# Sixty matrix products on constant tiles, appended at the end of a two-layer hybrid trunk

## The chip, the core and the metric

The kernel runs on one core of a Trainium2 chip. The metric is the device time of one execution in microseconds, as the median over executions of the program. A separate, profiled execution gives the trace; its span runs from the first to the last instruction, and its device time is somewhat longer than its span.

A core has a matrix engine (TensorE, PE in the profile; its weight loads stand in a row of their own, PEld), a vector engine (VectorE, DVE), an activation engine (ScalarE, ACT), a general engine (GpSimd, POOL) and one that issues transfers (SyncE, SP). ACT, POOL and SP issue DMA transfers here. A product reads a stationary operand (the weights that are loaded into the array, one column for each row of the output) and a moving operand that streams through, both from the on-chip memory SBUF, and writes or adds into a bank of the accumulator memory PSUM (512 fp32 values in each of 128 partitions).

## The reference

Two layers over 256 tokens of 2048 channels in fp32. Each has a convolution branch and an attention branch, both read from one input projection, merged by sigmoid gates and put through an output projection.

```python
def hybrid_layer(x, cos, sin, norm_g, w_in, ...):
    h = rmsnorm(x, norm_g)
    proj = h @ w_in
    (c_a, c_glu, c_gate, q_down, kv_down, k_pe, m_gate,
     g_conv, g_mla) = jnp.split(proj, idx, axis=-1)
    y_conv = conv_branch(c_a, c_glu, c_gate, ...) @ w_proj_conv
    y_mla = mla_branch(q_down, kv_down, k_pe, m_gate, cos, sin, ...) @ w_proj_mla
    y = jax.nn.sigmoid(g_conv) * y_conv + jax.nn.sigmoid(g_mla) * y_mla
    return x + y @ w_out
```

The appended products compute nothing of this: they read tiles of ones, and what they write into PSUM is read by nobody.

## The kernel before

Every large product splits each fp32 number into a high and a low part of type fp32r (`F32R` in the code) and adds three partial products: high by high, low by high, high by low. Weights come in pieces of 128 x 2 x 512 values (`raw`), ACT rounds them to `hi`, VectorE subtracts to get `lo`, and TensorE runs twelve products for a piece: two halves of the tokens, two blocks of 128 channels, three parts. The stationary operand is a 128 x 128 block of the activations (`h_hi`, `h_lo`, later `oT`, `ycT`, `yT`), the moving operand a 128 x 512 block of the weights. An instruction `matmul` on fp32r brings its own weight load, so each product is one MATMUL and one LDWEIGHTS in the profile.

The function `trunk` issues all of it. The wrapper `InOrder` around each engine (`pe`, `vec`, `act`, `gps`, `sp`) ties every instruction to the one issued before it on the same engine, so each engine runs its instructions in the order of the code. As all of them go through the wrapper's inner function `issue`, nearly all lines of the profile say L135. A step that belongs beside the products is put at a slot (`at_slot`, `late`, `fill`) and issued when `product` has issued the piece of that slot. The last kind of block is `wout`: four blocks of 512 output channels, 48 products of 128 x 512 for each half of the tokens. `wout_evac` of the last layer adds PSUM to the residual in `xres` on VectorE, 256 columns at a time; for the last block SP and ACT issue the output transfers. After `trunk` the program closes (L1407): SP waits for the last events of all engines and transfers, and then the engines meet.

Tiles come from pools that rotate over a fixed number of buffers for each tag: `uv` has nine buffers of 128 x 572 values, `big` six of 128 x 4096, and `s0` and `s1` one PSUM bank each, used by the attention scores. A new tile of a tag takes the oldest buffer of it and waits for its last readers.

Three things in the kernel are related to the appended work. At the very start, nineteen products `warm` of 256 columns run on a constant zero (both operands read one constant element, broadcast), and their result is never read. The score products `s` of the attention read both operands from one tile, `qk_t`. And the first block of the first layer takes its first two pieces in single blocks, so TensorE waits there between products.

Of the kernel before, what the change touches and what calls it, by code (L numbers as in the profile page):

```python
# [11 lines left out]
F32 = mybir.dt.float32  # L12
F32R = mybir.dt.float32r
# [6 lines left out]
P = 128  # L20
T = 2
SEQ = 256
# [4 lines left out]
PAD = CONV_W - 1  # L27
# [96 lines left out]
def trunk(ctx: ExitStack, tc: tile.TileContext, xT, x, g_in, pos, win, wuq, wukv, wpc, wpm, wo, cst, rows, invf, out):  # L124
# [411 lines left out]
    for l in range(DEPTH):  # L536
# [763 lines left out]
        if not last_layer:  # L1300
            h_hi, h_lo = keep["h"]

def _blocked(w, widths):
# [105 lines left out]
```

## Time and profile before

| | |
|---|---|
| median of 2 runs | 1876.24 us (1876.01 to 1876.46) |
| profiled execution | 1876.45 us |
| its span | 1874.7 us |
| granted TensorE clock, mean | 1.000 |
| matrix products, weight loads | 8571, 8571 |
| PE busy, of the span | 1869.2 us |
| VectorE busy, of the span | 1577.5 us |

Times are in microseconds unless marked ns. Lines of a group give the line of code, the engine, the operation, the tile written and the tiles read, the shapes, a count, and then the busy time, the mean duration of one in ns, and the idle time of the engine just before them with what ended it. The duration of a product is longer than the distance to the next one, because products are pipelined: the rate is read from the starts. In the chain of waits a line gives its start, its length and what it was; the timeline gives the same for each engine, with runs of like instructions merged and their count behind an x. In a table of windows each engine's busy time stands with its number of instructions, then the granted clock (1.00 is full speed), the share of the DMA engines and GB/s.

### The profile page before, as it was taken

How to read it: one execution, taken by the hardware profiler on the slowest of the kernel's cores; microseconds unless marked ns; L12 is line 12 of the kernel's file. 1: busy time of each engine (PE TensorE's matmuls, PEld its weight loads, DVE VectorE, ACT ScalarE, POOL GpSimd, SP SyncE). 2: the span in 40 equal slices, each digit the busy share in tenths (PEclk: the TensorE clock that was granted, in tenths of full speed). 3: DMA queues.
4: the chain of work that ended last, by engine and by line, in shares of the span. 5: the costliest groups of instructions: out<-in, count | busy, mean ns of one | idle time of the engine just before them, and what ended most of it. 6: DMA issues, size and time to landing. Idle time of an engine off the chain costs nothing.

```text
span 1874.7 us, 27153 instructions
## 1 busy us (share of the span) xinstructions
PE 1869.2 (100%) x8571; PEld 1570.0 (84%) x8571; DVE 1577.5 (84%) x2452; ACT 1358.2 (72%) x2510; POOL 493.7 (26%) x942
## 2 busy tenths in 40 slices
PE   9999999999999999999999999999999999999999
PEld 8988888888888888888899888888888888888887
DVE  6899998898999988766679899889899999885664
ACT  7678888888888876644557688788889888574442
POOL 1055555542200000122221455555322000001210
PEclk9999999999999999999999999999999999999999
DMA  9677777787755566678876777777777556566775
GB/s 327 218 261 257 263 255 256 259 275 232 235 203 193 198 205 218 207 240 277 291 233 218 257 268 254 261 255 269 256 237 242 192 192 204 208 205 223 237 251 164
DMA packets 138961, 445.05 MB, mean 237 GB/s; under 512 B 23681, under 2 KB 29313, under 8 KB 138817
## 3 DMA queue, kind: packets, MB, share of 16 engines
q1 hardware_dynamic: 105120, 359.89, 57.0%
q0 software_dynamic: 32832, 82.62, 13.8%
q8 instruction: 67, 1.10, 0.2%
q10 hardware_dynamic: 864, 0.80, 0.2%
q14 instruction: 78, 0.63, 0.1%
HBM read 399.18 MB, written 44.04 MB: 236 GB/s over the span
## 4 chain that ended last, share of the span: by engine, by line
PE 99%; DMA 1%; ACT 0%; DVE 0%; DVEq 0%; SPq 0%; issue 0%
PE acc L135 97%; PE s L135 2%; PE o_ps L135 1%; DMA raw<-in_win 0%; DMA gx<-in_g 0%; ACT hi L135 0%; PE var L135 0%; PE mu L135 0%; DVE xres L135 0%; DVEq L1407 0%; SPq L135 0%
## 5 line engine op out<-in xcount | busy, mean ns | idle before, releaser
L135 ACT CAST hi<-raw 128x1024 fp32r<-128x1024 f32 (+3 forms) x682 | 699.3, 1032 | 407.4 <-PE acc L135 350.3
L135 DVE TENSOR_TENSOR lo<-raw,hi 128x1024 fp32r<-128x1024 f32 (+3 forms) x682 | 814.1, 1195 | 192.7 <-PE acc L135 146.6
L135 PE MATMUL acc<-hi,hT 128*128 128x512 f32 (+2 forms) x1728 | 419.6, 382 | 0.0
L135 PEld LDWEIGHTS acc<-hi,hT 128*128 128x128 f32 x1728 | 319.6, 188 | 59.1
L135 PE MATMUL acc<-hi,h_hi 128*128 128x512 f32 (+2 forms) x864 | 260.5, 383 | 0.9 <-ACT hi L135 0.9
L135 PE MATMUL acc<-hi,h_lo 128*128 128x512 f32 (+2 forms) x864 | 260.1, 382 | 0.0
L135 ACT ACTIVATE tap<-u_t,cst 128x256 f32<-128x256 f32 x542 | 235.2, 499 | 2.8 <-DVE v_t L135 2.8
L135 PE MATMUL acc<-lo,h_hi 128*128 128x512 f32 (+2 forms) x864 | 229.7, 382 | 0.0
L135 PE MATMUL acc<-lo,hT 128*128 128x512 f32 (+2 forms) x864 | 229.3, 382 | 0.0
L135 DVE TENSOR_TENSOR v_t<-v_t,tap 128x512 f32<-128x512 f32 x271 | 186.3, 688 | 9.7 <-DVE v_t L135 0.9
L135 POOL DMA_DIRECT2D turned<-turn_d x88 | 49.2, 560 | 530.6 <-DVE v_t L135 311.8
L135 PEld LDWEIGHTS acc<-hi,h_lo 128*128 128x128 f32 x864 | 161.0, 188 | 30.2
L135 PEld LDWEIGHTS acc<-lo,h_hi 128*128 128x128 f32 x864 | 160.5, 188 | 30.2 <-DVE lo L135 0.3
L135 PEld LDWEIGHTS acc<-lo,hT 128*128 128x128 f32 x864 | 160.6, 188 | 30.0
L135 PEld LDWEIGHTS acc<-hi,h_hi 128*128 128x128 f32 x864 | 159.9, 188 | 30.6 <-ACT hi L135 1.9
L135 DVE SCALAR_TENSOR_TENSOR v_t<-u_t,cst,v_t 128x256 f32<-128x256 f32 x418 | 178.3, 479 | 2.0
L135 POOL DMA_DIRECT2D turn_d<-gate x184 | 100.2, 552 | 292.9 <-DVE gate L135 176.6
L135 PE MATMUL acc<-hi,oT 128*128 128x512 f32 x512 | 127.8, 389 | 0.0
L135 PE MATMUL acc<-hi,ycT 128*128 128x512 f32 x512 | 127.7, 389 | 0.0
L135 PE MATMUL acc<-hi,yT 128*128 128x512 f32 x512 | 127.7, 389 | 0.0
L135 PE MATMUL acc<-hi,qkc 128*128 128x512 f32 x448 | 115.4, 389 | 0.0
L135 PEld LDWEIGHTS acc<-hi,ycT 128*128 128x128 f32 x512 | 96.1, 188 | 20.0
(171 smaller groups left out, 2221.6 us busy)
## 6 DMA issues: line engine op xcount, KB each, us to landing
raw<-in_win SPq DMA_DIRECT2D x382, 512.0 KB, 4.1
raw<-in_wpm SPq DMA_DIRECT2D x64, 512.0 KB, 3.3
raw<-in_wpc SPq DMA_DIRECT2D x64, 512.0 KB, 4.2
raw<-in_wo SPq DMA_DIRECT2D x64, 512.0 KB, 4.8
raw<-in_wukv SPq DMA_DIRECT2D x32, 512.0 KB, 4.3
turned<-turn_d POOLq DMA_DIRECT2D x56, 256.0 KB, 4.7
raw<-in_win SPq DMA_DIRECT2D x32, 384.0 KB, 4.3
raw<-in_wuq SPq DMA_DIRECT2D x24, 512.0 KB, 4.4
```

The costliest lines, as they stand in the source:

```text
L135: ins = getattr(self.engine, name)(*a, **k)
```

## The change

Behind the last layer, still inside `trunk`, two tiles are taken and filled with ones by VectorE: `near`, a `uv` tile, and `far`, a `big` tile, of which the first 1024 and the last 1024 columns are written. Two PSUM banks are taken under the tags `s0` and `s1`. Then ten groups of six products follow, each with 512 moving columns:

1. weights `near`, 128 columns, banks in turn
2. the same, all six adding into one bank
3. weights of 64 columns, at a named place in the array, output in 64 partitions
4. the same with 32 columns and 32 partitions
5. weights one column of `near`, broadcast to 128
6. moving operand one column of `far`, broadcast to 512
7. both broadcast
8. weights in `far`, 3072 columns from the moving operand
9. weights in `far`, the first 128 of the moving columns themselves
10. weights in `far`, right behind the moving columns

Nothing else differs.

```diff
         if not last_layer:
             h_hi, h_lo = keep["h"]
 
+    near = uv_p.tile([P, 2, PAD + SEQ], F32R, tag="uv", name="near").rearrange("p j n -> p (j n)")
+    far = big.tile([P, 4096], F32R, tag="big", name="far")
+    vec.memset(near.bitcast(F32), 1.0)
+    vec.memset(far[:, :1024].bitcast(F32), 1.0)
+    vec.memset(far[:, 3072:].bitcast(F32), 1.0)
+    banks = [s_p.tile([P, 512], F32, tag=f"s{i}", name=f"bank{i}") for i in range(2)]
+    one, row = near[:, :1].broadcast_to([P, P]), far[:, :1].broadcast_to([P, 512])
+    there = far[:, 3072 : 3072 + P]
+
+    def six(stationary, moving, rows=P, chained=False):
+        kw = {} if rows == P else {"tile_position": (0, 0)}
+        for n in range(6):
+            pe.matmul(banks[0 if chained else n % 2][:rows], stationary, moving,
+                      start=n == 0 or not chained, stop=n == 5 or not chained, **kw)
+
+    six(near[:, :P], far[:, :512])
+    six(near[:, :P], far[:, :512], chained=True)
+    six(near[:, :64], far[:, :512], rows=64)
+    six(near[:, :32], far[:, :512], rows=32)
+    six(one, far[:, :512])
+    six(near[:, :P], row)
+    six(one, row)
+    six(there, far[:, :512])
+    six(far[:, :P], far[:, :512])
+    six(far[:, 512 : 512 + P], far[:, :512])
```

## The prediction

> **What bounds the kernel now.** I read the totals of the page first, then the chain of waits, then the last microseconds of the timeline.
>
> ```profile
> span 1874.7 us, 27153 instructions
> PE 1869.2 (100%) x8571; PEld 1570.0 (84%) x8571; DVE 1577.5 (84%) x2452; ACT 1358.2 (72%) x2510; POOL 493.7 (26%) x942
> PE 99%; DMA 1%; ACT 0%; DVE 0%; DVEq 0%; SPq 0%; issue 0%
> ...
> 10.56 1.05 ACT hi L135
> 11.66 164.66 PE acc L135 x804
> ...
> 257.84 24.50 PE acc L135 x108
> ...
> 1639.66 231.22 PE acc L135 x1020
> 1870.91 0.42 DVE xres L135
> 1871.34 0.33 DVEq L1407
> ```
>
> TensorE is the chain: 99% of it, from 11.66 us to the last output product. There is no gap on it into which sixty more products could be put, and they are issued behind the last one anyway. So the question is only what the end of the kernel looks like, because everything before it stays as it is.
>
> ```profile
> start us, us, engine line op out<-in xcount [idle before <-releaser]
> 1870.26 0.61 PE L135 MATMUL acc<-lo,yT 128*128 128x512 f32 x2
> 1870.46 1.24 SPq L135 DMA_DIRECT2D out<-xres  x2
> 1870.79 1.26 ACTq L135 DMA_DIRECT2D out<-xres  x2
> 1870.91 0.76 DVE L135 TENSOR_TENSOR xres<-acc,xres 128x256 f32<-128x256 f32 x2 [0.15 <-PE acc L135]
> ...
> L135 ACTq DMA_DIRECT2D out<-xres x2: 350/350/351, 1870.8 to 1871.7; - x2
> DMA to landing us min/median/max: 1.9/2.0/2.1
> ...
> L1407 SPq EVENT_SEMAPHORE  x12: 17/28/28, 1871.7 to 1874.6; - x12
> L1407 POOLq EVENT_SEMAPHORE  x4: 17/17/17, 1873.9 to 1874.5; - x4
> ```
>
> The first five lines are the timeline of the last microseconds; then come the page of the tile `xres` and the page of line 1407, which closes the program. TensorE is done at 1870.26 + 0.61 = 1870.87. VectorE adds the last block by 1870.91 + 0.76 = 1871.67. The last output transfer is issued at 1871.7 and lands 2.0 later, at 1873.7. Line 1407 waits for everything, then the engines meet: 1874.7 − 1873.7 = **1.0 us of closing** after the last event that it waits for. TensorE has nothing to do from 1870.87 on, and that tail is what the added work grows out of.
>
> **The change, part by part.** No DMA is added, so no queue of SP, ACT or POOL has anything behind it; the two output issues of SP and ACT stand ahead of all of this and only need the adds. Nothing is removed, and the new tiles have the sizes of the tiles whose buffers they take.
>
> *Three memsets on VectorE*, 572, 1024 and 1024 elements a partition. They are issued after the last add, so they begin at 1871.67. The first products read `near` and the first half of `far`, so TensorE waits for two of the three. No memset this wide is in the trace; these rows bound it:
>
> ```profile
> L135 DVE MEMSET ones<- 128x128 f32 x1 | 0.2, 165 | 0.8 <-PEq L1400 0.8
> L135 DVE MEMSET ss_base<- 128x4 f32 x2 | 0.1, 62 | 0.0
> L135 DVE COPY s1c<-v_t 128x512 f32<-128x512 f32 x2 | 0.9, 428 | 0.1
> L135 DVE CAST parts<-s1c 128x256 fp32r<-128x256 f32 x2 | 0.6, 294 | 0.1
> L135 DVE TENSOR_TENSOR lo<-raw,hi 128x1024 fp32r<-128x1024 f32 x630 | 767.8, 1220 | 172.6 <-PE acc L135 129.3 <-issue 20.3 <-ACT hi L135 9.9
> L135 DVE TENSOR_TENSOR lo<-raw,hi 128x512 fp32r<-128x512 f32 x4 | 2.8, 690 | 0.0
> ```
>
> The two memsets give (165 − 62) / 124 = 0.83 ns an element over a base of 62 ns: 62 + 568 × 0.83 = 533 ns for `near` and 62 + 1020 × 0.83 = 909 ns for half of `far`, 1.44 us together. The copies are faster an element, (428 − 294) / 256 = 0.52 ns, which makes 0.36 + 0.59 = 0.95 us; the subtractions slower, (1220 − 690) / 512 = 1.04 ns, which makes 0.65 + 1.12 = 1.77 us. I take 1.44, since it is the operation itself, and keep both ends. The third memset, 0.9 us, lies beside the first 42 products (over 9 us of TensorE work); only the eighth group reads it, so it costs nothing, and 0.9 us if that cover were gone.
>
> TensorE then starts 0.05 us after the second memset, as it did at 11.66 after ACT's 10.56 + 1.05 = 11.61: 1871.67 + 1.44 + 0.05 = 1873.16.
>
> *The sixty products.* All are 512 columns wide except that the output of twelve has fewer rows. The 108 products from 257.84 us took 24.50 us, 226.9 ns each, with a weight load for every one of them. What can differ is the operands:
>
> ```profile
> L135 PE MATMUL acc<-hi,yT 128*128 128x512 f32 x512 | 127.7, 389 | 0.0
> L135 PEld LDWEIGHTS acc<-hi,yT 128*128 128x128 f32 x512 | 96.1, 188 | 19.9
> 4.21 0.50 PE L135 MATMUL warm<-const-float32-0.0 128*128 128x256 f32 x3
> L135 PE MATMUL warm<-const-float32-0.0 x3: 273/274/274, 4.2 to 4.4; 128*128 128x256 f32 x3
> 283.35 0.88 PE L135 MATMUL s<-qk_t 128*128 128x256 f32 x6
> L135 PE MATMUL s<-qk_t x8: 278/283/288, 283.1 to 283.9; 128*128 128x256 f32 x8
> 11.66 0.73 PE L135 MATMUL acc<-hi,h_hi 128*128 128x512 f32 x2 [0.38 <-ACT hi L135]
> 12.23 0.40 PE L135 MATMUL acc<-hi,h_lo 128*128 128x512 f32 x1
> ```
>
> A load takes 188 ns and lies wholly beside the product before it, so 64 or 32 columns in place of 128 shorten something that is hidden. The score products `s` have both operands in one tile, `qk_t`: (0.88 − 0.283) / 5 = 119 ns for 256 columns. The `warm` products have one constant as both operands, a broadcast that overlaps itself: (0.50 − 0.274) / 2 = 113 ns, 6 ns less. From 256 to 512 columns an interval grows from 119 to 227, 108 ns, so 512 columns are 215 ns of streaming and some 12 ns of something else, which is all that a narrow load or a broadcast could save. Five of the ten groups have one: 30 × 12 ns = 0.36 us at the most. I take 0 and keep 0.36 for the low end. Groups eight to ten (weights in the tile of the moving operand: far away, overlapping, next to it) I cost as the plain ones by the `s` and `warm` rows; if such reads did collide so far that the load was exposed, 188 ns × 18 = 3.4 us would come on top.
>
> The narrow groups are the one thing without a row: the outputs of 64 and 32 rows name a place in the array, so there are three changes of shape (128 to 64, to 32, back). A change costs nothing if the array doesn't care; if it empties first, a product outlasts the next one's start by 389 − 227 = 162 ns, and with the next load exposed as well 162 + 188 = 350 ns. That makes 0, 0.49 or 1.05 us for three. I take 0.25, the middle of the first two, as the loads of every row here overlap. The Trainium skill (TensorEngine Tiling, Key Properties) has a rule against it: changing the tiling mode drains the engine. By that rule alone the sum would be 0.24 us higher, and no trace here shows such a change.
>
> Sum: 59 intervals × 0.2269 = 13.39 us; the first product after a wait has a slower start, 0.73 us for the first pair at 11.66 against 0.61 for the pair at 1870.26, so 0.12; the last one runs its 0.389 to the end; 0.25 for the changes. 14.15 us from 1873.16 gives 1887.31. The closing then takes its 1.0 us: **1888.3, that is 13.6 us more span.** The output transfers have landed by 1873.7, far inside.
>
> The profiled execution took 1876.45 us with this span, so the changed one takes 1890.05. Its 1876.45 is 0.21 above the median of the runs, 1876.24; I forecast **1890.0 us**.
>
> **The rivals.** *The clock drops in the gap.* TensorE stands still from 1870.87 to 1873.16, 2.3 us, the longest gap in the program.
>
> ```profile
> core 0: us, PE busy (x) PEld busy (x) DVE busy (x) ACT busy (x) POOL busy (x), PEclk, DMA share, GB/s
> 1870.90:1874.50 3.60, 0.00 (x0) 0.00 (x0) 0.76 (x2) 0.00 (x0) 0.00 (x0) 1.00 0.44 146
> 1874.60:1874.70 0.10, 0.00 (x0) 0.00 (x0) 0.00 (x0) 0.00 (x0) 0.00 (x0) 0.50 0.00 0
> ...
> 0.75:4.00 3.25, 3.22 (x15) 3.25 (x16) 1.00 0.57 131
> ```
>
> At the end of the old kernel the granted clock was still 1.00 at 1874.50 and 0.50 at 1874.60, some 3.7 us after the last product. With 2.3 us the gap stays short of that, unless the drop comes at fixed times and counts a partly idle stretch. The first `warm` products show the price of a slow array: 3.22 us for 15 of 256 columns is 215 ns each, twice the 113. So one stretch of 3.3 us at that rate would hold 7 to 8 of the new products and cost 0.2 us each: +1.6 us, two stretches +3.1 us, giving 1891.6 to 1893.1. The Trainium skill (TensorE: Matmul & The Clock Gate, Why this matters for your kernels) asks for no idle gap above about 3 us, which agrees with the 3.7 us here and also clears this gap.
>
> *The narrow outputs lose the single pass.* If an output that doesn't fill the array made TensorE run a product in four passes, twelve products would gain three streams of 215 ns: 12 × 0.645 = +7.7 us, 1897.7. For it: no narrow product is in the trace. Against it: nothing else about type or width changes.
>
> *All sixty run in four passes* and the kernel ends slower by over 2%: 60 × 0.645 = +38.7, 1928.7. It decides from the point where 2% (37.5 us, about what a measurement of this kernel can tell from no change) is passed: 1890.05 − 1876.24 = 13.8 of them are spent already, 23.7 are left, so 37 of the sixty at four passes. The plain products have type and shape of the 226.9 ns ones, so at most the odd groups (48) could do it; nothing in the profile does.
>
> *The products aren't there.* Nobody reads their result. If they were dropped, only the memsets would stay, 1871.67 + 1.44 + 0.9 = 1874.0 against the 1873.7 of the transfers: +0.3, 1876.6. But nobody reads the nineteen `warm` products either, and they are in the trace.
>
> **How the numbers follow.** Forecast 0.80, clock drop 0.12, narrow products in four passes 0.05, products dropped 0.02, all in four passes 0.01. The forecast's own bounds: memsets −0.5 or +0.3, shape changes −0.25 or +0.8, narrow loads and broadcasts −0.36, and the closing or the execution by some 0.2 either way: 1888.7 to 1891.3. The range takes in the clock drop, the next case above, and rounds outward: 1888.5 to 1893.1; it leaves out the four passes and the dropped products. Faster by over 2%: no case has it, 0. Slower by over 2%: only the last, 0.01. Within 2%: the rest, 0.99.
>
> **What would show it.** VectorE: three memsets right after the last `xres` add, two of them near 1.44 us together. TensorE: a gap of about 2.3 us, then sixty products at 227 ns, granted clock 1.00 throughout; the ten groups differ by no more than 14 ns a product, with a larger step only at the two edges and the return of the narrow groups. The closing at line 1407: still about 1.0 us after the last product. The prediction is wrong if a group of six takes more than 1.6 us, if the clock shows 0.50 in the added stretch, or if anything before 1870 us moved.

## The result: 15.8 us more, and a clock that fell behind the gap

The changed kernel takes 1892.01 us (two executions, 1891.72 and 1892.29) against 1876.24 before: a ratio of 1.0085, 95% interval 1.0068 to 1.0101. The profiled execution took 1891.72 us with a span of 1889.9.

The totals of the changed kernel's page and its two lines on the chain of waits:

```profile
span 1889.9 us, 27276 instructions
PE 1884.7 (100%) x8631; PEld 1581.4 (84%) x8631; DVE 1580.4 (84%) x2455; ACT 1358.5 (72%) x2510; POOL 494.0 (26%) x942
PE 99%; DMA 0%; DVE 0%; ACT 0%; issue 0%; DVEq 0%; SPq 0%
PE acc L135 96%; PE s L135 2%; PE o_ps L135 1%; PE bank L135 1%; DMA raw<-in_win 0%; DMA gx<-in_g 0%; ACT hi L135 0%; DVE far L135 0%; DVE near L135 0%; PE var L135 0%; PE mu L135 0%; DVE xres L135 0%; DVEq L1433 0%; SPq L135 0%
```

Sixty products and three VectorE instructions are there, and `bank` is a new 1% of the chain. The old part ends at the same place: the chain of the last microseconds (start, length, what) has the last add at 1870.98, 0.07 us later than before.

```profile
1870.98 0.42 DVE xres L135
1871.41 0.33 DVEq L1433
1871.74 0.07 issue
1871.80 0.54 DVE near L135
1872.34 0.16 issue
1872.50 0.92 DVE far L135
1873.43 0.04 issue
1873.47 15.52 PE bank L135 x60
```

The memsets last what was forecast (0.54 and 0.92), but there is 0.07 us ahead of the first and 0.16 between them. The sixty take 15.52 us, not 14.15. A table of windows of the same execution says where:

```profile
1870.90:1873.40 2.50, 0.04 (x1) 0.00 (x0) 2.19 (x4) 0.00 (x0) 0.00 (x0) 1.00 0.63 210
1873.50:1874.50 1.00, 1.00 (x4) 0.83 (x5) 0.91 (x1) 0.00 (x0) 0.00 (x0) 1.00 0.00 0
1874.60:1877.90 3.30, 3.30 (x10) 2.45 (x9) 0.00 (x0) 0.00 (x0) 0.00 (x0) 0.50 0.00 0
1878.00:1889.00 11.00, 10.99 (x49) 8.04 (x47) 0.00 (x0) 0.00 (x0) 0.00 (x0) 1.00 0.01 1
```

The sixth column after the window's length is the granted clock: 1.00 while the first four products ran, then 0.50 for one stretch, then 1.00 again. The trace records the changes themselves: down at 1874.57, 1.1 us after the products had begun, and up at 1877.99, 3.41 us later. Inside that stretch a product takes 427 ns, start to start. Seven whole ones and two partly slow ones cost 7 × 200 + 128 + 77 = 1.6 us. This is the rival "the clock drops in the gap", at its price of +1.6 us and its time of 1891.6, though the drop itself came behind the gap.

### The profile page after: what moved, and what is told of

Same layout as the page of the kernel before. It is cut to its first block, busy times and chain, and to the rows that moved or that the text cites. A ratio compares the mean times of both kernels' runs of the same rounds, so it can differ in the third digit from the quotient of the medians.

```text
span 1889.9 us, 27276 instructions
## 1 busy us (share of the span) xinstructions
PE 1884.7 (100%) x8631; PEld 1581.4 (84%) x8631; DVE 1580.4 (84%) x2455; ACT 1358.5 (72%) x2510; POOL 494.0 (26%) x942
## 4 chain that ended last, share of the span: by engine, by line
PE 99%; DMA 0%; DVE 0%; ACT 0%; issue 0%; DVEq 0%; SPq 0%
PE acc L135 96%; PE s L135 2%; PE o_ps L135 1%; PE bank L135 1%; DMA raw<-in_win 0%; DMA gx<-in_g 0%; ACT hi L135 0%; DVE far L135 0%; DVE near L135 0%; PE var L135 0%; PE mu L135 0%; DVE xres L135 0%; DVEq L1433 0%; SPq L135 0%
## 5 line engine op out<-in xcount | busy, mean ns | idle before, releaser
L135 PEld LDWEIGHTS acc<-hi,oT 128*128 128x128 f32 x512 | 96.1, 188 | 20.0
```

Of the source, the lines that this page charges most:

```text
L135: ins = getattr(self.engine, name)(*a, **k)
```

## The experiments

**Does the gap bring the clock down, or do the sixty products?** Four kernels on one chip. `early` fills the two tiles before the third of the last four output blocks:

```diff
                 wout_begin(i)
+                if last_layer and i == 2:
+                    constant["near"] = uv_p.tile([P, 2, PAD + SEQ], F32R, tag="uv", name="near")...
+                    constant["far"] = big.tile([P, 4096], F32R, tag="big", name="far")
+                    vec.memset(constant["near"].bitcast(F32), 1.0)
...
```

> The two tiles are filled before the third of the four last output blocks, while VectorE has slack, so TensorE goes from the last output product straight to the sixty. Theory: the granted clock fell to 0.50 because TensorE stood still for 2.5 us; without that gap it stays at 1.00, the sixty take 13.5 to 13.7 us, and the time is about 1887.3 us. Rival: the added products themselves (constant operands) bring the clock down; then it still shows 0.50 for 3.4 us and the time is about 1888.9 us. If the 231 ns intervals come from the addresses, groups 1 to 5, 8 and 9 keep 231 ns; if they are a state that the disturbance left behind, they show 227 ns.

`early` took 1887.0 us (1886.63 to 1887.38), ratio 1.0057 (1.0042 to 1.0072), and all four executions have a mean clock of 1.000. The chain's last piece:

```profile
1871.03 13.63 PE bank L135 x60
```

The sixty follow the output block at once and stay at full speed, constant operands and all: no product stands more than 235 ns from the next.

`filled` and `half_filled` leave the memsets where the change has them and put zero products into the gap, 22 and 11 of them:

```diff
+    idle = tp_p.tile([P, 256], F32, tag="tp", name="idle")
+    for i in range(22):
+        pe.matmul(idle, zeros[:, :P], zeros, start=i == 0, stop=i == 21)
     banks = [s_p.tile([P, 512], F32, tag=f"s{i}", name=f"bank{i}") for i in range(2)]
```

> The memsets stay where the change has them, but 22 products of 256 columns on the constant zero are put on TensorE ahead of the sixty, 113 ns each by the trace of before, 2.5 us, which fills the gap. Theory (the clock fell for the gap): the clock stays at 1.00, the sixty start at the same 1873.5 us and the time is the changed kernel's minus 1.6, about 1890.4 us. Rival (the sixty bring the clock down): 1892.0 us as before, with 0.50 from about 1874.6 us.

> The same with 11 of these products, so that TensorE works until about 1872.2 us and stands still for 1.3 us before the sixty. If the clock looks at fixed stretches of 3.41 us and needs one of them mostly idle, the stretch from 1871.16 to 1874.57 us is now about 60% busy, the clock stays at 1.00 and the time is 1890.4 us. If a shorter gap is enough, it falls at 1874.57 us again and the time is 1892.0 us.

`filled` (22 products) took 1889.84 us (1889.52 to 1890.37), `half_filled` (11) 1890.1 us (1889.51 to 1890.54); each has four executions, all with a mean clock of 1.000. So products in the gap, even in half of it, take the drop away, though work is added; the rival that the sixty bring the clock down falls.

**Why did two executions of two drop, when the gap is shorter than 3.7 us?** The changed kernel again, and one with a longer gap, in which the second and third memset change places so that the products wait for all three:

```diff
-    vec.memset(far[:, :1024].bitcast(F32), 1.0)
     vec.memset(far[:, 3072:].bitcast(F32), 1.0)
+    vec.memset(far[:, :1024].bitcast(F32), 1.0)
```

> The changed kernel itself, unedited, in more executions. If the clock looks at fixed stretches of 3.41 us that lie differently against the program from one execution to the next, a gap of 2.5 us fits into one stretch in only a part of them: some executions come out near 1890.3 us (no drop) and some near 1891.9 us. If the stretches lie always the same, or if any gap of this length is enough, all executions lie between 1891.6 and 1892.4 us.

> The second and third memset change places, so the sixty wait for all three and TensorE stands still for 3.6 us in place of 2.5. The sixty start 1.07 us later. If the half clock lasts one stretch of 3.41 us in any case, the time is the changed kernel's plus 1.1, 1893.1 us. If the clock comes back only some 4.5 us after TensorE resumes, as it did in the changed kernel, another 0.5 us is added, 1893.6 us. Without a drop it would be 1891.4 us.

`again` came out at 1889.72, 1890.17, 1890.98, 1891.08 and 1891.11 us. The first two of these have a mean clock of 1.000, the other three of 0.999. So the 15.8 us of the result belongs to two executions that both dropped; over all seven the median is 1891.08. The profiled one here is that of 1890.17; the last piece of its chain:

```profile
1873.52 13.92 PE bank L135 x60
```

and two of its windows:

```profile
1870.90:1873.40 2.50, 0.09 (x1) 0.00 (x0) 2.14 (x4) 0.00 (x0) 0.00 (x0) 1.00 0.63 210
1874.60:1877.90 3.30, 3.30 (x16) 2.28 (x15) 0.00 (x0) 0.00 (x0) 0.00 (x0) 1.00 0.00 0
```

The same code and the same empty 2.5 us, and no drop: sixteen products where the other execution had ten. `longer_gap` gave 1891.12 us with a mean clock of 1.000, and 1892.29, 1892.57 and 1893.3 with 0.999. The first of these is in the profile:

```profile
1870.90:1874.40 3.50, 0.00 (x0) 0.00 (x0) 3.10 (x5) 0.00 (x0) 0.00 (x0) 1.00 0.45 150
1874.60:1877.90 3.30, 3.30 (x15) 2.55 (x16) 0.00 (x0) 0.00 (x0) 0.00 (x0) 1.00 0.00 0
```

Even 3.6 us of standing still left the clock up there, while 2.5 us brought it down elsewhere. So the length of the gap alone doesn't decide; where it falls in a beat of the chip's own does, and the traces show that beat. In the changed kernel's profile the clock goes up at 4.068 us and down at 1874.572, which is 548 times 3.4133 us later; it is up again one such step later. In all nine traces that record changes of the clock (27 behind the first ones), each lies a whole number of such steps behind the first, while the first lies anywhere between 3.83 and 6.62 us. The Trainium skill (TensorE: Matmul & The Clock Gate, Part 1) states such a beat: a free-running window of 3413 ns. These traces agree with it.

With the beat laid out from the first change, the steps that hold the gap are, for the changed kernel (and the step behind it), for `again` (two), for `longer_gap` (two) and for `half_filled`:

```profile
1871.16:1874.57 3.41, 1.10 (x5) 0.93 (x6) 2.94 (x5) 0.00 (x0) 0.00 (x0) 1.00 0.46 154
1874.57:1877.98 3.41, 3.41 (x10) 2.56 (x9) 0.00 (x0) 0.00 (x0) 0.00 (x0) 0.50 0.00 0
...
1869.20:1872.61 3.41, 1.79 (x8) 1.13 (x7) 2.11 (x6) 0.00 (x0) 0.00 (x0) 1.00 0.31 102
1872.61:1876.02 3.41, 2.50 (x11) 2.09 (x12) 1.76 (x2) 0.00 (x0) 0.00 (x0) 1.00 0.15 52
...
1869.31:1872.72 3.41, 1.56 (x7) 0.94 (x6) 2.34 (x6) 0.00 (x0) 0.00 (x0) 1.00 0.38 125
1872.72:1876.13 3.41, 1.66 (x7) 1.40 (x8) 1.53 (x2) 0.00 (x0) 0.00 (x0) 1.00 0.08 29
...
1870.45:1873.86 3.41, 2.13 (x15) 1.78 (x14) 2.96 (x6) 0.00 (x0) 0.00 (x0) 1.00 0.46 154
```

The first number behind the length is the time that TensorE was busy. In the changed kernel nearly the whole gap fell into one step, which was 32% busy, and the clock fell at its end. In `again` and `longer_gap` an edge cut the gap in two: the steps were 52% and 73% busy, or 46% and 49%, and the clock stayed. The profile of `half_filled` has nearly the whole gap in one step again; with its eleven products the step is 62% busy, without them it would have been 26%. Over the traces, each of the 18 steps at full clock that were 34% busy or less ends with the clock falling, and none of 45% or more does; what happens between isn't settled. By these shares an estimate is that a gap of 2.53 us drops the clock in 43 to 65% of its places in the beat, 3.6 us in 74 to 96%, 1.3 us in none; counted by mean clocks the runs had 5 of 7, 3 of 4 and 0 of 4.

Two cautions. Ahead of the first recorded change, and in a trace that records none (`early`, `filled`, `half_filled`, `longer_gap`, `moving_patterns`), the clock's column prints 1.00 whatever the clock was; there the distances of the products tell. So the beat of `longer_gap` and `half_filled` is an estimate, from where their first products change from 427 to 227 ns (5.64 and 6.77 us; the same reading comes within 0.03 us of the recorded change in six other traces). And a mean clock of 0.999 is what one step at 0.50 makes (two would make 0.998), so the three other executions of `longer_gap` had one step of half clock as well; none of them has a trace. Their 1892.3 to 1893.3 us lie at or below the 1893.1 expected for one.

**The tail without the products.** `memsets_only` leaves out the banks and the sixty products.

> The sixty products and their banks are left out; the three memsets stay. VectorE ends at about 1874.5 us, 0.7 us after the last output transfer has landed, and the closing takes its 1.0 us from there: span 1875.4 us, time 1877.0 us. If the memsets delayed anything of the old kernel, the time is higher.

`memsets_only` took 1877.13 us, ratio 1.0005 (0.9996 to 1.0014), so not to be told from no change. In its trace VectorE ends at 1873.04 + 0.91 = 1873.95, and the span of 1875.0 is 1.05 behind it. That end was expected at 1874.5; it came earlier as the whole execution did, whose last product ends at 1870.41, 0.53 us earlier than in the changed kernel.

**Do the group times belong to the operands?** The start-to-start distances of the ten groups, in ns, as means of the records of six products (five for the last):

```
group                      changed  again   early   reversed
1  near, banks in turn        (a)    (b)    226.7    226.8
2  near, one bank           426.7   226.5   226.7    230.5
3  64 weight columns          (a)   229.7   229.7    229.8
4  32 weight columns        231.5   231.5   231.3    231.0
5  broadcast weights        232.0   232.2   232.3    231.7
6  broadcast moving         218.2   218.2   218.0    218.8
7  both broadcast           218.7   218.7   218.7    218.3
8  weights far away         231.0   231.0   231.0    226.5
9  weights overlapping      230.2   230.0   230.2    226.7
10 weights right behind     226.6   226.8   226.6    226.8
(a) partly at half clock   (b) 335 for the first, then 228 to 236
```

`early_reversed` runs the groups from the tenth to the first (this kernel and the three behind it, `long_groups`, `moving_patterns` and `turns`, were executed once each):

> As the kernel with early memsets, with the ten groups in reversed order. If the 231 ns intervals belong to the addresses of weights and moving operand, each group keeps its number: 227 for the weights right behind the moving columns, 231 for the others, 218 for the broadcast moving operand. If they are a state of TensorE that a disturbance leaves and that wears off, the first groups run at 227 ns whichever they are. The narrow groups run as the wide ones if a change of shape costs nothing.

Groups 8 and 9 fall from 231 to 227 when they come ahead of the narrow ones, so the place of the weights in SBUF, overlapping ones too, costs nothing; the second group now shows 230.5, since it follows the narrow ones. Longer groups tell the rest:

```diff
-    six(near[:, :P], far[:, :512])
...
+    run(24, near, wide)
+    run(24, near, wide, rows=(64,))
+    run(24, near, wide, rows=(32,))
+    run(24, near, wide)
+    run(24, one, wide)
+    run(12, near, row)
+    run(24, near, wide)
+    run(24, near, wide, rows=(P, 64, 32))
+    run(12, near, wide)
+    run(24, near, far[:, :P], width=P)
+    run(24, near, far[:, :P], rows=(64,), width=P)
+    run(24, near, far[:, :P], rows=(32,), width=P)
```

> The memsets are early, and in place of the sixty stand longer groups: 24 plain, 24 with 64 weight columns, 24 with 32, 24 plain, 24 with broadcast weights, 12 with broadcast moving operand, 24 plain, 24 with 128, 64 and 32 weight columns in turn, 12 plain; then 24 each of 128, 64 and 32 weight columns against 128 moving columns. If 231 ns is a state that wears off, a group that starts at 231 ns ends at 227 ns; if narrow loads and broadcast weights cost 4 to 5 ns themselves, they keep 231 ns to the end. Changing the shape at every product: 227 to 235 ns if it costs nothing, 389 ns if the array empties first. Against 128 moving columns a load of 128 columns isn't hidden any more, about 115 ns a product; loads of 64 and 32 columns then give about 66 ns.

From the timeline of `long_groups`, where a mixed group stands under the shape of one of its products: 64 columns, 32 columns, plain ones behind them, three shapes in turn, then 128, 64 and 32 weight columns against 128 moving ones.

```profile
1875.95 5.22 PE L135 MATMUL bank<-far,near 128*64 128x512 f32 x22
1881.47 5.26 PE L135 MATMUL bank<-far,near 128*32 128x512 f32 x22
...
1887.95 4.47 PE L135 MATMUL bank<-far,near 128*128 128x512 f32 x19
...
1906.10 5.48 PE L135 MATMUL bank<-far,near 128*64 128x512 f32 x23
...
1914.20 2.62 PE L135 MATMUL bank<-far,near 128*128 128x128 f32 x22
1916.84 1.48 PE L135 MATMUL bank<-far,near 128*64 128x128 f32 x22
1918.39 1.31 PE L135 MATMUL bank<-far,near 128*32 128x128 f32 x19
```

With the last one's 0.39 us taken off, 22 products with 64 columns stand (5.22 − 0.39) / 21 = 230 ns apart, with 32 columns 232 ns, to the end of their groups; plain ones behind them are back at (4.47 − 0.39) / 18 = 227 ns after four products. So there are both: narrow loads cost 3 to 5 ns each as long as they last, and plain ones need some products to settle. A change of shape at every product makes (5.48 − 0.39) / 22 = 231 ns, where an array that empties first would show 389, so nothing drains. Against 128 moving columns the load counts, start to start in the records: 112 ns with 128 weight columns, 60 ns with 64, and 60 with 32, so that a still shorter load gains nothing.

**What is the broadcast moving operand spared?** Groups of twelve with plain weights and other moving operands, 512 columns each:

```diff
-    six(near[:, :P], far[:, :512])
...
+    run(12, near, far[:, :512])
+    run(12, near, row)
+    for n in (2, 4, 16, 64, 256):
+        run(12, near, far[:, :n].unsqueeze(1).broadcast_to([P, 512 // n, n]))
+    run(12, near, far[:, :256].unsqueeze(2).broadcast_to([P, 256, 2]))
+    run(12, near, far[:, :512].rearrange("p (a b) -> p b a", a=2))
+    run(12, near, far[:, 1:513])
+    run(12, near, far[:, 0:1024:2])
...
```

> The memsets are early, and in place of the sixty stand groups of twelve with plain weights and other moving operands of 512 columns: the plain one; one column broadcast; runs of 2, 4, 16, 64 and 256 columns repeated; each of 256 columns twice; two halves interleaved; the plain one shifted by one column; every second of 1024 columns; the plain one again; then 64 weight columns without and with a named place in the array. Broadcasting one column saved 8 ns a product. If that is because only one address is read, the runs go up from 218 to 227 ns with their number of columns; if a single repeated column is a case of its own, all of them take 227 ns. A step of two or interleaving takes 227 ns if each column costs the same wherever it lies, and more, up to twice, if neighbours are read together. The 64-column loads take 230 ns both times if the named place doesn't matter.

In ns, as means without the first interval of a group: plain 226.7; one column 218.9; runs of 2, 4, 16, 64, 256 columns repeated 218.7, 218.6, 242.3, 230.5, 226.7; each column twice 215.8; **two halves in turn 215.8**; shifted by one column 237.3; a step of two 454.0; 64 weight columns 229.4 with and without the named place. The timeline's pieces for plain, two halves in turn, and a step of two:

```profile
1870.55 2.43 PE L135 MATMUL bank<-far,near 128*128 128x512 f32 x10
...
1891.67 2.75 PE L135 MATMUL bank<-far,near 128*128 128x512 f32 x12
...
1897.33 5.62 PE L135 MATMUL bank<-far,near 128*128 128x512 f32 x12
```

Two halves in turn read all 512 columns and still take less than one column broadcast, and 11 ns less than the plain order: (2.75 − 0.38) / 11 = 215.5 ns against (2.43 − 0.39) / 9 = 226.7. That was foreseen by neither theory, so more orders were measured:

```diff
+    turns = lambda x, a: x.rearrange("p (a b) -> p b a", a=a)
+    run(12, near, turns(wide, 2))
+    run(12, near, turns(wide, 4))
+    run(12, near, turns(wide, 8))
+    run(12, near, wide.rearrange("p (a b c) -> p b a c", a=2, c=2))
+    run(12, near, wide.rearrange("p (a b c) -> p b a c", a=2, c=4))
+    run(12, near, wide.rearrange("p (g a b) -> p g b a", a=2, b=4))
...
```

> Early memsets, and in place of the sixty groups of twelve: plain; two halves in turn; four quarters in turn; eight eighths in turn; two halves in turn by runs of 2 and of 4 columns; pairs of columns 4 apart in turn; two halves in turn shifted by one column; plain shifted by 2 and by 4 columns; two halves in turn with 64 weight columns and with broadcast weights; plain and two halves in turn with 256 columns. If leaving the column's neighbour is what helps, all of the first kind take 216 ns, the runs of 2 and 4 go up to 227. If it is the two places far apart, pairs 4 apart take 227 and four or eight places more than 216. If the shift of one column costs its 10 ns only because a group of neighbours is cut, the interleaved shifted group keeps 216, and a plain shift by 4 costs nothing. If narrow and broadcast weights cost 4 to 5 ns through the moving read, they take 216 as well; 256 columns fall from 119 to 109 ns.

In ns: two halves in turn 215.8; four quarters 283.3; eight eighths 489.6; two halves by runs of 2 columns 328.0, of 4 columns 252.0; pairs 4 columns apart 215.8; two halves shifted by one column 216.6; plain shifted by 2 columns 233.5, by 4 columns 231.0; two halves with 64 weight columns 215.9, with broadcast weights 215.9; 256 columns 118.4 plain and 111.7 in two halves. Two halves, four quarters, pairs 4 apart, and two halves with 64 weight columns in the timeline:

```profile
1874.07 2.32 PE L135 MATMUL bank<-far,near 128*128 128x512 f32 x10
1876.72 3.00 PE L135 MATMUL bank<-far,near 128*128 128x512 f32 x10
...
1892.94 2.32 PE L135 MATMUL bank<-far,near 128*128 128x512 f32 x10
...
1903.70 2.32 PE L135 MATMUL bank<-far,near 128*64 128x512 f32 x10
```

The distance doesn't matter between 4 and 256 columns; two places in strict turn do. They also take away the shift's 10 ns and the narrow load's 3 ns.

**Does the kernel's own stream gain from it?** In the kernel before, without the appended work, the even columns of each weight block are laid ahead of the odd ones in memory, and the product reads the two halves in turn, so that the output's order stays:

```diff
                 pe.matmul(
-                    pts[t][:, :n], stationary, w[:, kk, :],
+                    pts[t][:, :n].rearrange("p (b a) -> p b a", a=2), stationary,
+                    w[:, kk, :].rearrange("p (a b) -> p b a", a=2),
...
         b = w[:, at : at + n].reshape(k, KS, P, n).transpose(0, 2, 1, 3)
+        b = b[..., np.arange(n).reshape(n // 2, 2).T.reshape(-1)]
```

> The kernel before, without the appended work, with one thing changed: each block of weights lies in memory with its even columns ahead of its odd ones, and every large product reads its moving operand from the two halves in turn, so that the output comes out in the old order. Theory: a product of 512 columns takes 216 ns in place of 227 in the kernel's own stream too, with real data and with the weight loads, so 8256 products give up to 90 us back, less where VectorE sets the pace (it was 97% busy between 500 and 600 us): between 1786 and 1840 us. Rival: the saving belongs to constant tiles or to an idle machine; then the time stays at 1876 us. Another: the interleaved reads meet other engines' accesses and the products get slower.

> The same, and the planner's estimate of a slot, 12 times (columns / 2400 + 0.0133) us, gets 0.0025 for 0.0133, so that the convolution work on VectorE is dealt out for the shorter slots. If VectorE held the products back in the kernel with the old estimate, this one is faster by the part of the 90 us that was lost there, towards 1786 us. If the convolution work is then left over and run in a burst ahead of the convolution's projection, it is slower than the one with the old estimate.

`interleaved` takes **1798.9 us (1798.71 to 1799.22), ratio 0.9588 (0.9574 to 0.9602)**: 77 us less than before. From its page:

```profile
span 1797.2 us, 27159 instructions
PE 1786.2 (99%) x8571; PEld 1572.5 (87%) x8571; DVE 1565.1 (87%) x2452; ACT 1345.9 (75%) x2510; POOL 495.3 (28%) x942
PE 82%; DVE 6%; issue 4%; DMA 3%; ACT 3%; POOL 2%; DVEq 0%; POOLq 0%; ACTq 0%
```

A piece of its chain:

```profile
247.23 23.31 PE acc L135 x108
```

And TensorE's waits that cost most (total, times, longest):

```profile
PE acc L135 <- DVE su L135: 2.7, 6, 0.6
PE acc L135 <- ACT junk L135: 2.0, 3, 0.7
```

The 108 products that took 24.50 us take 23.31, 215.8 ns each, so the saving isn't one of constant tiles or of an idle machine. The share of TensorE on the chain goes from 99% to 82%, as waits for other engines that were hidden now come out. In the records the 512-column products of `acc` that stand over 20 ns farther apart than the rest lose some 13 us together, against 1 before; that is about the rest of the 90 us. `interleaved_paced`, with the shorter slot estimate, takes 1875.21 us, ratio 0.9996 (0.9986 to 1.0006). Its waits of TensorE, and a step of the beat in such a wait with the stretch behind it:

```profile
PE acc L135 <- ACT ycT L135: 51.5, 8, 11.6
PE var L135 <- DVE parts L135: 12.8, 1, 12.8
...
730.14:733.55 3.41, 0.00 (x0) 0.00 (x0) 3.41 (x7) 1.63 (x3) 0.00 (x0) 1.00 0.05 20
733.56:757.44 23.88, 4.33 (x10) 3.18 (x11) 18.86 (x36) 12.99 (x20) 2.19 (x4) 0.50 0.21 66
```

The planner dealt out less convolution work per slot, it was left over, and the convolution's projection waited for it eight times: the burst of the expectation. The waits make 64 us of the 76 by which it is slower than `interleaved`. The clock adds to them: all ten executions have a mean of 0.980 to 0.982, and this trace has eight stretches of half clock ahead of its end, 68.7 us in all. TensorE was busy for 37.5 us of them, which at full clock would have been about half, some 19 us less.

## Why the prediction came out as it did

The forecast was 1890.0 us in a range of 1888.5 to 1893.1. The median of 1892.01 lies in the range, in the case that had a chance of 0.12; the likeliest case, at 0.80, had no drop. By its own signs this forecast failed: the clock shows 0.50 in the added stretch, and the second group of six takes 6 × 0.427 = 2.6 us, where 1.6 was the bound. The sum itself gives 1889.84, as the 0.21 us between the profiled execution and the median was named but not taken off. That the two executions without a drop, 1889.72 and 1890.17, lie so close to it is partly luck: 0.30 us of pauses and later start were missing from the sum, and 0.23 us too much stood in it for the sixty.

- *What stays as it is.* Right: the old part ends 0.07 us later, and the closing takes 1889.9 − (1873.47 + 15.52) = 0.9 us for a forecast 1.0.
- *Memsets.* 0.535 and 0.912 us for forecast 0.533 and 0.909. Missing were the pauses of 0.07 and 0.16 us, so the sixty began at 1873.47 and not at 1873.16; 0.07 of that is the later end of the old part.
- *The sixty at full clock.* 13.92 us in `again` for a forecast 14.15. The difference is the 0.25 for three changes of shape, which cost nothing: products stand 231 ns apart even when each has another shape. The Trainium skill's rule on tiling modes (TensorEngine Tiling, Key Properties), weighed there, shows no cost at this change, where outputs of 128, 64 and 32 rows begin at the same place; other places and row tiles weren't tried.
- *Loads, broadcasts, places.* The bound of 12 ns held: broadcasting the moving operand saves 8. Narrow loads and broadcast weights were taken as possible gains and cost 3 to 6 ns instead. Over `early` the twelve products with a broadcast moving operand save 0.10 us and the thirty of groups 3, 4, 5, 8 and 9 cost 0.13 us, so they nearly cancel.
- *The clock.* Here the forecast's likeliest case failed, in the step "With 2.3 us the gap stays short of that, unless the drop comes at fixed times and counts a partly idle stretch". The exception that it names is what happened. The 3.7 us at the end of the old kernel was no threshold but the wait for the end of the first step of the beat that lay wholly behind the last product (1871.17 to 1874.58), and a step that was 32% busy was enough. Of the seven executions of the changed kernel five show a mean clock of 0.999 and took 1890.98 us or more; the two without are 1889.72 and 1890.17, around the forecast 1890.0. The price was right for the profiled execution; the three of `again` with a drop are 1.1 us above the two without, perhaps as part of their slow step lay in the gap, which no trace shows.
- *The other rivals.* No group ran in four passes, and no product was dropped. Without the products the time is 1877.13 and not 1876.6: in `memsets_only` VectorE ends 1873.95 − 1870.41 = 3.54 us behind the last product, by the same pauses, where the prediction had 1874.0 − 1870.87 = 3.1.

## What to carry to other kernels

A gap of TensorE costs more than its length when it leaves a step of the clock's own beat mostly empty (34% busy or less here): put the preparing instructions (here three memsets) ahead of the last dense work, or spare products into half of the gap. A drop that was seen once in a trace gives no threshold; the spread over several executions, with their mean clocks, tells more than one profile, and the steps of the beat, laid out from the first change of clock in a trace, tell why. And the order in which a moving operand is read is worth measuring alone: two places in turn, prepared in the layout of the weights, took 4.1% off a kernel whose chain was 99% TensorE.

## What the runs showed of the hardware that was not expected

- An fp32r product of 512 columns read in order takes 226.7 ns, in two interleaved halves 215.8, with four places in turn 283, with eight 490, with a step of two 454. For 256 columns it is 118.4 and 111.7. The Trainium skill (TensorE: Matmul & The Clock Gate, Back-to-back issue gap) gives N / 2.4 + 2.5 ns for the isolated gap of a warm array, by which an estimate is 215.8 for 512 and 109.2 for 256. The interleaved products agree at 512 and are 2.5 ns above it at 256; the plain ones are 11 and 9 ns above. Why two places in turn are read better than neighbours wasn't found.
- A moving operand that starts one column later costs 10.6 ns a product, two columns later 6.8, four columns later 4.3.
- The same code with the same gap runs with and without a stretch of half clock from execution to execution, in `again` 1891.06 and 1889.95 us on the mean. The changes of clock lie on a beat of 3.4133 us that starts at another point in each execution, and a step that is 34% busy or less is enough to bring the clock down.
- After a stall or a narrow load the plain products run at 224 to 236 ns for some four to ten products before they settle at 226.7.
